# Decode's convolution rows on ScalarE's queue, and a last norm summed on two engines with whole-row stores

## The chip, the cores and the metric

The kernel runs on one core of a Trainium2 chip. The core has TensorE for matrix products (PE in the profile; its weight loads are PEld), VectorE (DVE), ScalarE (ACT), GpSimd (POOL) and SyncE (SP), and 16 DMA engines that all queues share. The metric is the device time of one execution in microseconds; 0.3% of it is about 8 us. Each engine works through its own list of instructions in order; a transfer is started by an instruction in the list ("queue") of the engine that issues it, here SyncE, ScalarE or GpSimd.

## What is computed

One step of a small hybrid decoder with two layers: 1040 prompt tokens (16 learned meta tokens and 1024 of the prompt) and 8 decode tokens, model width 1024. Layer 0 has a causal convolution of width 31, layer 1 an RWKV-7 time mixing; each is followed by a squared-ReLU MLP of width 4096. Two parts of the reference matter here, the convolution's state and the final norm:

```
def _conformer_conv(h, buf, ...):
    u = h @ w_pw1 + b_pw1
    u = u[..., :D_MODEL] * jax.nn.sigmoid(u[..., D_MODEL:])
    full = jnp.concatenate([buf.astype(u.dtype), u], axis=1)
    c = lax.conv_general_dilated(full, w_dw[:, None, :], ...) + b_dw
    ...
    return out, full[:, -CONV_BUF:]

def _rmsnorm(x, g):
    y = xf * lax.rsqrt(jnp.mean(xf * xf, axis=-1, keepdims=True) + RMS_EPS)
    return (y * g.astype(jnp.float32)).astype(x.dtype)

    return (_rmsnorm(h, norm_final), ...)
```

For each of the 8 decode sequences the new convolution state is the old one's last 29 rows, each of 1024 numbers, and one new row. `y_prompt` and `y_sample` are the final norm's output, without the meta tokens.

## The kernel before

All activations lie with channels on the 128 partitions: a tile `h` of `[128, 8, n]` holds 1024 channels (8 tiles of 128, index `k` or `m`) of `n` tokens. The tokens are cut into groups, three for layer 0 (`G0`, 352, 348, 348 tokens), four for the time mixing, and three for the last stage (`G2`: 328, 352, 352 tokens, the meta tokens left out). Matrix products with the big weights are done as three products of split operands (`mm3`, lines 186 to 190): the high part of the weights times the high part of the activations, low times high, and high times low. So each weight block of 512 KB is loaded by SyncE into one of five `raw` buffers (`load_raw`, line 147), copied by ScalarE to its high part (line 158), and GpSimd subtracts to get the low part (line 163). Loads are issued as buffers come free.

The MLP (`mlp`, lines 319 to 388) walks over 32 blocks of the hidden width. For a block `j`, `inp` makes `ps_in` on PE, VectorE scales it (line 343), ScalarE squares it (344) and casts the high part `hh` (141), VectorE makes the low part `hl` (142). For two blocks together, `out` makes eight products `out` that VectorE adds to the residual `h` (355). PE thus needs ScalarE's weight casts and its `hh` all the time.

Between the PE work of the MLP, `filler` hands out other work in portions: generators yield a number for the work they have just traced, and each call of `fill` takes as much as the call's share of a budget. In layer 0's group 0 such a stream is `conv_states` and `conv_dec` (line 549): decode's convolution. `conv_dec` loads the old states of four sequences at a time into a tile `sdec` (line 553; 120 rows of 4 KB on 120 partitions), and then for each `m` transposes them on PE (`pw`, line 559), copies them to `win` on ScalarE (561), multiplies (563), sums (566) and adds the bias (567). In the same loop body, and with no other tie to it than the loop, one sequence's 29 rows are stored to the output from `sdec` (line 564); such a store waits only for the load of its `sdec`.

The planner of the framework works out the order of the instructions of each engine ahead of the run, from the order in which they are traced, their dependences and its own estimate of times; an instruction that is ready may go ahead of earlier ones that are not. In a few sections the order of one engine is fixed by hand (`manual_schedule`): TensorE's in the time mixing and the first group of the last stage, VectorE's in layer 0's last group.

The last stage ends as follows. Group 0 is done on its own; groups 1 and 2 share the weight loads of one MLP. When group 1's last `out` is traced, `done(1)` makes its final norm, `final(1)`, the filler of group 2's last products; `final(2)` comes after everything. `final(g)` (line 1574) sums the squares of the 1024 channels of each token, multiplies `h` by the norm's weights (1587, 1589), transposes to rows of tokens on PE (`pf`, 1613), scales each row by its reciprocal root on ScalarE or VectorE while it is moved to `ot` (1616, 1618), and stores. A group has three blocks of up to 128 tokens. For group 0 the squares are summed by `mean_parts` (line 217): ScalarE squares the eight tiles, GpSimd adds the four even ones and VectorE the four odd ones, and PE sums the two results over the partitions with a column of ones (`fs`, line 1597). For groups 1 and 2 ScalarE writes eight square tiles `fq` (1585), and PE sums all eight over the partitions, 8 matmuls a block. The rows are stored in halves of 512 columns, each after its own eviction (1620 for the prompt, 1622 for the decode tokens, which are in group 2's last block).

Of the kernel before, what the change touches and what calls it, by code (L numbers as in the profile page):

```python
# [8 lines left out]
F32 = mybir.dt.float32  # L9
F32R = mybir.dt.float32r  # L10
BF16 = mybir.dt.bfloat16
AF = mybir.ActivationFunctionType
# [4 lines left out]
P = 128  # L17
D = 1024
KT = D // P
# [7 lines left out]
CB = CW - 1  # L27
# [21 lines left out]
def hybrid_step(tc, x_prompt, x_sample, state_conv, state_shift, state_wkv, meta_tokens,  # L49
# [8 lines left out]
    nc = tc.nc  # L58
    ctx = ExitStack()
    with ctx:  # L60
        def pool(stack, name, bufs, **kw):
            return stack.enter_context(tc.tile_pool(name=name, bufs=bufs, reuse_waits="tile", **kw))
# [4 lines left out]
        ones_d = consts.tile([P, P], F32, name="ones_d")  # L67
# [41 lines left out]
        for name, ap in vecs:  # L109
            n = ap.shape[0]  # L110
# [7 lines left out]
        def vec(name, i):  # L118
            c = col[name] + i
            return pvec[:, c:c + 1]  # L120

        cur = {}
# [7 lines left out]
        def stat(name, tag, bufs, w=None):  # L130
            return cur["stat"].tile([P, w or cur["n"]], F32, name=name, tag=tag, bufs=bufs)
# [60 lines left out]
        def bank(name, tag="mm"):  # L192
            return cur[tag].tile([P, 512], F32, name=name, tag=tag)
# [20 lines left out]
        def tt(name, tag):  # L214
            return cur["tmp"].tile([P, cur["n"]], F32, name=name, tag=tag)

        def mean_parts(src, n, name, square, tag="acc"):

            accs = []
            for i, eng in enumerate((nc.gpsimd, nc.vector)):  # L220
                acc = stat(f"acc_{name}{i}", f"{tag}{i}", 1)
                ks = range(i, KT, 2)
                for j, k in enumerate(ks):
                    if square:
                        d = tt(f"sq_{name}{k}", "t1") if j else acc
                        nc.scalar.activation(d[:, :n], src[:, k, :n], AF.Square)
                        d = d[:, :n]
                    else:
                        d = src[:, k, :n]
                    if j:  # L230
                        eng.tensor_add(acc[:, :n], acc[:, :n] if square or j > 1 else src[:, ks[0], :n], d)
                accs.append(acc)
            return accs
# [156 lines left out]
        with ExitStack() as l0:  # L390
# [6 lines left out]
            actp = [pool(l0, f"actp0{i}", 1) for i in range(2)]  # L397
# [151 lines left out]
            def conv_dec(c, c_col):  # L549

                sd = [decp.tile([P, D], F32, name=f"sdec{i}", tag="st", bufs=2)[:4 * CB, :] for i in range(2)]
                for i in range(2):
                    nc.sync.dma_start(sd[i], state_conv[0, 4 * i:4 * i + 4].rearrange("b w d -> (b w) d"))
                yield 1
                for m in range(KT):
                    win = decp.tile([P, DEC, CW], F32, name=f"win{m}", tag="win")
                    ps = bank(f"pw{m}", "x")
                    for i in range(2):
                        nc.tensor.transpose(ps[:, i * 4 * CB:(i + 1) * 4 * CB], sd[i][:, m * P:(m + 1) * P],
                                            ident[:4 * CB, :4 * CB])  # L560
                    nc.scalar.copy(win[:, :, :CB], ps[:, :DEC * CB].rearrange("p (b w) -> p b w", b=DEC))
                    nc.gpsimd.tensor_copy(win[:, :, CB:CW], udec[:, m, :].unsqueeze(2))
                    nc.vector.tensor_mul(win, win, wdw[:, m:m + 1, :].broadcast_to([P, DEC, CW]))
                    nc.sync.dma_start(o_conv_sample[0, m, 0:CB - 1, :], sd[m // 4][m % 4 * CB + 1:(m % 4 + 1) * CB])
                    rd = decp.tile([P, DEC], F32, name=f"rd{m}", tag="rd")
                    nc.vector.tensor_reduce(rd, win, axis=AX.X, op=ALU.add)
                    nc.scalar.activation(c[:, m, c_col:c_col + DEC], rd, AF.Identity, bias=vec("b_dw", m))
                    yield 1
# [116 lines left out]
            with ExitStack() as s:  # L685
# [39 lines left out]
                for i, parts in enumerate((((1, rwkv_w1[0]), (4, rwkv_a1[0])), ((5, rwkv_g1[0]),))):  # L725
                    own, prev = (xin.tile([P, D], F32, name=f"lr{i}{s_}", tag="xt").rearrange("p (k c) -> p k c", k=KT) for s_ in "op")
                    w = P // len(parts)
                    for q, (j, src) in enumerate(parts):
                        cs = slice(q * w, (q + 1) * w)
# [84 lines left out]
        wide = pool(ld, "wided", 4)  # L814
# [722 lines left out]
        with ExitStack() as l1:  # L1537
            open_tmp(l1, N2, "2", 3, False)
            open_weights(l1, 0, {"w": 5}, "f")
            actp = pool(l1, "actp1", 1)  # L1540
# [33 lines left out]
            def final(g):  # L1574
                lo, n = G2[g]
                hv = hl[g][:, :, :n]
                if g:
                    accs = [(actp, actp2)[g - 1].tile([P, cur["wide"]], F32R, name=f"fq{g}{k}", tag=f"acth{k}").bitcast(F32)
                            for k in range(KT)]
                else:  # L1580
                    accs = mean_parts(hv, n, f"f{g}", True, "facc")
                    yield 3
                for k in range(KT):
                    if g:
                        nc.scalar.activation(accs[k][:, :n], hv[:, k, :], AF.Square)
                    if k % 2:
                        nc.scalar.activation(hv[:, k, :], hv[:, k, :], AF.Copy, scale=vec("norm_final", k))
                    else:
                        nc.vector.tensor_scalar(hv[:, k, :], hv[:, k, :], vec("norm_final", k), None, op0=ALU.mult)
                    if k == 3:  # L1590
                        yield 2
                starts = range(0, n, P)
                ps = bank(f"fs{g}", "x")
                for j, i in enumerate(starts):
                    w = min(P, n - i)
                    for q, acc in enumerate(accs):
                        nc.tensor.matmul(ps[:w, j:j + 1], acc[:, i:i + w], ones_d[:, 0:1], start=q == 0, stop=q == len(accs) - 1)  # L1597
                ss = stat(f"os{g}", "os", 1, 4)
                whole = n // P
                for w, js in ((P, slice(0, whole)), (n % P, slice(whole, len(starts)))):  # L1600
                    if js.stop > js.start:
                        nc.scalar.activation(ss[:w, js], ps[:w, js], AF.Sqrt, bias=eps_t[:w, 0:1])
                        nc.vector.reciprocal(ss[:w, js], ss[:w, js])
                yield 2
                for j, i in enumerate(starts):
                    w = min(P, n - i)
                    c = lo - META + i
                    np_ = max(0, min(w, SEQ - c))
                    ot = (outp if g < 2 else cur["raw"]).tile([P, D], F32, name=f"ot{g}_{i}", tag="raw")
                    for hf in range(2):  # L1610
                        pt = bank(f"pf{g}{i}{hf}", "w" if g < 2 or hf else "mm")
                        for q in range(4):
                            nc.tensor.transpose(pt[:w, q * P:(q + 1) * P], hv[:, hf * 4 + q, i:i + w], ident)
                        cs = slice(hf * 512, (hf + 1) * 512)
                        if hf:
                            nc.scalar.activation(ot[:w, cs], pt[:w, :], AF.Copy, scale=ss[:w, j:j + 1])
                        else:
                            nc.vector.tensor_scalar(ot[:w, cs], pt[:w, :], ss[:w, j:j + 1], None, op0=ALU.mult)
                        if np_:
                            nc.sync.dma_start(o_y_prompt[0, c:c + np_, cs], ot[:np_, cs])  # L1620
                        if np_ < w:
                            nc.sync.dma_start(o_y_sample.rearrange("b t d -> (b t) d")[:, cs], ot[np_:w, cs])
                    yield 5

            def until(last):
# [35 lines left out]
            residp2, actp2, hidp2 = pool(l1, "resid2", 2, **right), pool(l1, "actp2", 1, **right), pool(l1, "hidp2", 2, **right)  # L1661
# [3 lines left out]
            for _ in rest:  # L1665
                pass
            g1 = group(1, actp, hidp, sums)
            fill, rest = filler(2 * KT + MLP2_POINTS, ([ranked(FN, final(0))], FB))
            add, sums = sums_of(2)
            mixer_out(2, residp2, actp2, fill, add)  # L1670
            end = []

            def done(g):
                end.append(filler(KT, ([final(g)], 24)))
# [4 lines left out]
            for it in (rest, end[0][1], final(2)):  # L1679
                for _ in it:  # L1680
                    pass
# [31 lines left out]
```

## Time and profile before

| | us |
|---|---|
| median of 3 runs | 2752.41 |
| lowest and highest run | 2744.53, 2752.92 |
| profiled execution | 2749.91 |
| its span | 2748.2 |
| PE busy | 2641.3 |
| PEld busy | 2480.3 |
| VectorE busy | 1716.6 |
| GpSimd busy | 1443.8 |
| ScalarE busy | 1122.1 |

The profiled execution's time is 1.7 us longer than its span, from the first recorded event to the last. A timeline row gives start and duration in us, engine, line of the kernel, operation, output and inputs with their shapes, a count, and in brackets the engine's idle time before it and what ended it. SPq, ACTq and POOLq are the queues in which an engine's transfers are issued; the duration of such a row is how long the issue held that queue, not how long the transfer took. A matmul in this number format is recorded as one or several passes, and a row with a count merges neighbours.

### The profile page before, as it was taken

The numbers are of one execution on the slowest core, as the hardware profiler recorded it, in microseconds if no ns is written. First come the engines' busy times: TensorE is split into PE (matmuls) and PEld (weight loads), VectorE is DVE, ScalarE is ACT, GpSimd is POOL, SyncE is SP. The second block draws the span as 40 slices with busy tenths as digits, with TensorE's granted clock in tenths as the row PEclk, the third lists the DMA queues.
The fourth block names the chain that finished last, engine by engine and source line by source line (L and its number), as shares of the span: only waits on it lengthen the run. The fifth ranks groups of instructions, "written<-read, shape, count | busy, mean of one in ns | idle before, by whom it ended". The sixth has DMA issues, their size and how long they took to land. (4 is left out here: it accounts for less than half of the span.)

```text
span 2748.2 us, 51718 instructions
## 1 busy us (share of the span) xinstructions
PE 2641.3 (96%) x19948; PEld 2480.3 (90%) x19948; DVE 1716.6 (62%) x3546; ACT 1122.1 (41%) x2095; POOL 1443.8 (53%) x2054
## 2 busy tenths in 40 slices
PE   8999799999999999999999999979999999999998
PEld 8999699999999999877787787769999899999998
DVE  6999699997445345244757457576679753344433
ACT  5546345444444333333434444444543532222222
POOL 6678578878878776022111112365678663333330
PEclk9999899999999999999999999989999999999999
DMA  6663444554447442667777787786776642222211
GB/s 183 172 187 109 130 139 122 157 172 142 138 139 208 138 139 85 199 191 194 200 188 206 190 195 174 186 219 163 193 224 182 168 131 71 69 70 70 70 47 43
DMA packets 625548, 412.30 MB, mean 150 GB/s; under 512 B 121679, under 2 KB 567311, under 8 KB 625301
## 3 DMA queue, kind: packets, MB, share of 16 engines
q1 hardware_dynamic: 544643, 359.55, 46.7%
q10 hardware_dynamic: 72130, 23.61, 4.1%
q0 software_dynamic: 8528, 25.83, 2.9%
q8 instruction: 157, 2.57, 0.4%
q14 instruction: 90, 0.74, 0.1%
HBM read 344.81 MB, written 64.07 MB: 149 GB/s over the span
## 5 line engine op out<-in xcount | busy, mean ns | idle before, releaser
L163 POOL TENSOR_TENSOR wo_lo<-wo_raw,wo_hi 128x256 fp32r<-128x256 f32 x736 | 544.1, 772 | 318.7 <-ACT wo_hi L158 315.7
L163 POOL TENSOR_TENSOR wi_lo<-wi_raw,wi_hi 128x256 fp32r<-128x256 f32 x640 | 472.2, 770 | 264.8 <-ACT wi_hi L158 257.3
L188 PE MATMUL out<-hh,wo_hi 128*128 128x352 f32 (+2 forms) x1536 | 502.1, 327 | 20.3 <-DVE hl L142 13.3
L190 PE MATMUL ps_in<-m_l,wi_hi 128*128 128x352 f32 (+2 forms) x1536 | 494.2, 322 | 4.9 <-DVE m_l L286 4.8
L188 PE MATMUL ps_in<-m_h,wi_hi 128*128 128x352 f32 (+2 forms) x1536 | 495.4, 323 | 0.6 <-ACT m_h L285 0.6
L189 PE MATMUL out<-hh,wo_lo 128*128 128x352 f32 (+2 forms) x1536 | 495.6, 323 | 0.0
L190 PE MATMUL out<-hl,wo_hi 128*128 128x352 f32 (+2 forms) x1536 | 494.6, 323 | 0.0
L189 PE MATMUL ps_in<-m_h,wi_lo 128*128 128x352 f32 (+2 forms) x1536 | 491.9, 320 | 0.0
L355 DVE TENSOR_TENSOR h<-h,out 128x352 f32<-128x352 f32 (+2 forms) x768 | 385.7, 511 | 163.9 <-PE out L190 161.8
L536 DVE SCALAR_TENSOR_TENSOR cv<-u,wdw,cv 128x348 f32<-128x348 f32 (+2 forms) x720 | 377.9, 574 | 0.7
L158 ACT CAST wo_hi<-wo_raw 128x1024 fp32r<-128x1024 f32 x184 | 192.8, 1048 | 342.8 <-PE out L190 165.8
L158 ACT CAST wi_hi<-wi_raw 128x1024 fp32r<-128x1024 f32 x160 | 167.7, 1048 | 396.4 <-PE out L190 197.5
L188 PEld LDWEIGHTS out<-hh,wo_hi 128*128 128x128 f32 x1536 | 292.5, 190 | 27.3 <-DVE hl L142 15.4
L190 PEld LDWEIGHTS ps_in<-m_l,wi_hi 128*128 128x128 f32 x1536 | 288.8, 188 | 9.1 <-DVE m_l L286 8.6
L189 PEld LDWEIGHTS out<-hh,wo_lo 128*128 128x128 f32 x1536 | 291.7, 190 | 0.8
L188 PEld LDWEIGHTS ps_in<-m_h,wi_hi 128*128 128x128 f32 x1536 | 289.8, 189 | 2.6 <-ACT m_h L285 1.1
L190 PEld LDWEIGHTS out<-hl,wo_hi 128*128 128x128 f32 x1536 | 290.8, 189 | 0.2 <-DVE hl L142 0.2
L189 PEld LDWEIGHTS ps_in<-m_h,wi_lo 128*128 128x128 f32 x1536 | 289.2, 188 | 0.7
L343 DVE SCALAR_TENSOR_TENSOR ps_in<-ps_in,rs_m 128x352 f32<-128x352 f32 (+2 forms) x192 | 100.5, 524 | 247.6 <-PE ps_in L190 247.2
L142 DVE TENSOR_TENSOR hl<-ps_in,hh 128x352 fp32r<-128x352 f32 (+2 forms) x192 | 98.7, 515 | 139.7 <-ACT hh L141 139.6
L906 PE MATMUL pv<-mx,wv_raw 128*128 128x256 f32 (+2 forms) x512 | 133.1, 406 | 6.7 <-ACT rk L1082 4.7
L344 ACT ACTIVATE ps_in<-ps_in 128x352 f32<-128x352 f32 (+2 forms) x192 | 85.1, 444 | 132.1 <-DVE ps_in L343 131.7
(363 smaller groups left out, 4701.5 us busy)
## 6 DMA issues: line engine op xcount, KB each, us to landing
wi_raw<-in_w_mlp_in_dram SPq DMA_DIRECT2D x160, 512.0 KB
wo_raw<-in_w_mlp_out_dram SPq DMA_DIRECT2D x160, 512.0 KB
wk_raw<-in_rwkv_w_k_dram SPq DMA_DIRECT2D x32, 512.0 KB
wr_raw<-in_rwkv_w_r_dram SPq DMA_DIRECT2D x32, 512.0 KB
wv_raw<-in_rwkv_w_v_dram SPq DMA_DIRECT2D x32, 512.0 KB
d_ab<-ab POOLq DMA_DIRECT2D x32, 512.0 KB, 4.9
pg_raw<-in_conv_w_pw_dram SPq DMA_DIRECT2D x24, 512.0 KB
pa_raw<-in_conv_w_pw_dram SPq DMA_DIRECT2D x24, 512.0 KB
```

What stands on the lines that cost most here:

```text
L142: eng_lo.tensor_sub(lo, src, hi.bitcast(F32))
L158: nc.scalar.copy(hi[:, :a * b], raw[:, :a * b])
L163: eng_lo.tensor_sub(lo[:, cs], raw[:, cs], hi[:, cs].bitcast(F32))
L188: nc.tensor.matmul(ps, w[0], act[0], start=first, stop=False)
L189: nc.tensor.matmul(ps, w[1], act[0], start=False, stop=False)
L190: nc.tensor.matmul(ps, w[0], act[1], start=False, stop=last)
L343: nc.vector.scalar_tensor_tensor(s, s, 0.0, rs()[:, :n], op0=ALU.max, op1=ALU.mult)
L344: nc.scalar.activation(s, s, AF.Square)
L355: nc.vector.tensor_add(hv[:, 4 * i + m, :], hv[:, 4 * i + m, :], ps[:, :n])
L536: nc.vector.scalar_tensor_tensor(acc[m][:, :n], ug[:, m, j:j + n], wdw[:, m, j:j + 1], acc[m][:, :n], op0=ALU.mult, op1=ALU.add)
L906: nc.tensor.matmul(ps[:, :n], w[:, k, :], act[k], start=k == 0, stop=k == KT - 1)
```

## The change

Three edits. In `conv_dec` the store of a sequence's 29 rows is issued by ScalarE and not by SyncE. In `final` groups 1 and 2 sum their squares as group 0 does, with `mean_parts`, so that two accumulated tiles are left for PE and not eight; a `yield 3` behind it is now taken for every group. And a block's rows are stored whole, once both halves are in `ot`.

```
@@ conv_dec
-                    nc.sync.dma_start(o_conv_sample[0, m, 0:CB - 1, :], sd[m // 4][m % 4 * CB + 1:(m % 4 + 1) * CB])
+                    nc.scalar.dma_start(o_conv_sample[0, m, 0:CB - 1, :], sd[m // 4][m % 4 * CB + 1:(m % 4 + 1) * CB])
@@ final
-                if g:
-                    accs = [(actp, actp2)[g - 1].tile([P, cur["wide"]], F32R, name=f"fq{g}{k}", tag=f"acth{k}").bitcast(F32)
-                            for k in range(KT)]
-                else:
-                    accs = mean_parts(hv, n, f"f{g}", True, "facc")
-                    yield 3
+                accs = mean_parts(hv, n, f"f{g}", True, "facc")
+                yield 3
                 for k in range(KT):
-                    if g:
-                        nc.scalar.activation(accs[k][:, :n], hv[:, k, :], AF.Square)
                     if k % 2:
...
-                        nc.tensor.matmul(ps[:w, j:j + 1], acc[:, i:i + w], ones_d[:, 0:1], start=q == 0, stop=q == len(accs) - 1)
+                        nc.tensor.matmul(ps[:w, j:j + 1], acc[:, i:i + w], ones_d[:, 0:1], start=q == 0, stop=q == 1)
...
-                        if np_:
-                            nc.sync.dma_start(o_y_prompt[0, c:c + np_, cs], ot[:np_, cs])
-                        if np_ < w:
-                            nc.sync.dma_start(o_y_sample.rearrange("b t d -> (b t) d")[:, cs], ot[np_:w, cs])
+                    if np_:
+                        nc.sync.dma_start(o_y_prompt[0, c:c + np_, :], ot[:np_, :])
+                    if np_ < w:
+                        nc.sync.dma_start(o_y_sample.rearrange("b t d -> (b t) d"), ot[np_:w, :])
```

`mean_parts`, which the change calls for all groups (`tt(..., "t1")` is one of three buffers, `stat` one buffer a tag):

```
        def mean_parts(src, n, name, square, tag="acc"):
            accs = []
            for i, eng in enumerate((nc.gpsimd, nc.vector)):
                acc = stat(f"acc_{name}{i}", f"{tag}{i}", 1)
                ks = range(i, KT, 2)
                for j, k in enumerate(ks):
                    if square:
                        d = tt(f"sq_{name}{k}", "t1") if j else acc
                        nc.scalar.activation(d[:, :n], src[:, k, :n], AF.Square)
                        d = d[:, :n]
...
                    if j:
                        eng.tensor_add(acc[:, :n], acc[:, :n] if square or j > 1 else src[:, ks[0], :n], d)
                accs.append(acc)
            return accs
```

## The prediction

> **What bounds the kernel now.** I read the page first: span 2748.2 us, and the shares of the engines. TensorE's matmul row is 96% busy, so nearly everything that is moved on other engines is covered by it, and the change can only be worth something where TensorE stands still or does the work that is taken away.
>
> ```profile
> span 2748.2 us, 51718 instructions
> PE 2641.3 (96%) x19948; PEld 2480.3 (90%) x19948; DVE 1716.6 (62%) x3546; ACT 1122.1 (41%) x2095; POOL 1443.8 (53%) x2054
> PE   8999799999999999999999999979999999999998
> ```
>
> Idle PE is 2748.2 − 2641.3 = 107 us in the whole span, and the slices show one early hole: the fifth (275 to 344 us) is a 7. That is where decode's convolution rows are stored. Next I read the timelines of SyncE's queue, ScalarE and PE there, then the busy times by window.
>
> ```profile
> 292.93 3.28 SPq L564 DMA_DIRECT2D out_dram<-sdec  x3
> 296.32 4.98 SPq L147 DMA_DIRECT2D wi_raw<-in_w_mlp_in_dram  x1
> 301.35 14.54 SPq L564 DMA_DIRECT2D out_dram<-sdec  x4
> 316.00 7.01 SPq L147 DMA_DIRECT2D wo_raw<-in_w_mlp_out_dram  x2
> ...
> SPq L564 <- DMA sdec<-in_state_conv_dram: 3.0, 1, 3.0
> ...
> 306.69 0.34 ACT L561 COPY win<-pw 128x240 f32<-128x240 f32 x1
> 316.26 1.04 ACT L158 CAST wi_hi<-wi_raw 128x1024 fp32r<-128x1024 f32 x1 [9.23 <-PE pw L559]
> ...
> 317.69 0.45 ACT L141 CAST hh<-ps_in 128x352 fp32r<-128x352 f32 x1
> 335.49 1.04 ACT L158 CAST wo_hi<-wo_raw 128x1024 fp32r<-128x1024 f32 x1 [17.35 <-DMA wo_raw<-in_w_mlp_out_dram]
> ...
> 318.75 0.43 PE L188 MATMUL out<-hh,wo_hi 128*128 128x352 f32 x1 [2.61 <-DVE hl L142]
> ...
> 320.90 0.66 PE L188 MATMUL out<-hh,wo_hi 128*128 128x352 f32 x1 [0.91 <-DVE h L355]
> ...
> 337.88 0.66 PE L559 MATMUL pw<-ident,sdec 120*128 120x120 f32 x2 [14.85 <-ACT win L561]
> ...
> 320.50:341.00 20.50, 5.25 (x18) 4.79 (x19) 6.08 (x14) 3.25 (x6) 4.39 (x7) 0.50 0.49 146
> ```
>
> The eight stores of line 564 hold SyncE's queue: the last four for 14.54 us. The weight loads behind them start late and land late, ScalarE stands 17.35 us at the head of its queue for `wo_raw`, and PE idles 2.61 + 0.91 + 14.85 = 18.4 us. Columns of the last row are PE, PEld, DVE, ACT, POOL busy, granted clock, DMA share, GB/s: the clock is 0.50 for the 20.5 us that follow, so its 18 matmuls take 5.25 us where about 0.16 us each (2.9 us) would do: 2.3 us more. **The hole costs 20.7 us.** Why the stores are slow stands in the DMA view of 305 to 313 us, in which almost nothing but them runs:
>
> ```profile
> DMA packets 55, 0.23 MB, mean 29 GB/s; under 512 B 2, under 2 KB 2, under 8 KB 54
> q1 hardware_dynamic: 54, 0.21, 6.5%
> ```
>
> 6.5% of 16 engines is 1.04 engines: each store of 29 rows runs on one engine, 54 packets of mostly 4 KB in 8 us, about 0.155 us a row, so 4.5 us a store and 36 us for eight. Weight loads queue behind them for their share on that engine.
>
> At the other end I read the last 30 us on PE, ScalarE, VectorE and SyncE's queue.
>
> ```profile
> 2716.79 3.42 PE L1597 MATMUL fs<-ones_d,fq 128*128 128x1 f32 x34
> ...
> 2735.60 0.73 PE L1613 MATMUL pf<-ident,h 128*96 128x128 f32 x5
> 2736.17 3.43 PE L1597 MATMUL fs<-ones_d,fq 128*128 128x1 f32 x34
> ...
> 2733.27 0.91 ACT L1585 ACTIVATE fq<-h 128x352 f32<-128x352 f32 x2
> ...
> 2739.63 0.41 ACT L1602 ACTIVATE os<-fs,eps_t 128x2 f32<-128x2 f32 x2 [4.83 <-PE fs L1597]
> ...
> 2741.70 0.74 DVE L1618 TENSOR_SCALAR ot<-pf,os 96x512 f32<-96x512 f32 x1
> ...
> 2732.26 11.14 SPq L1620 DMA_DIRECT2D out_dram<-ot  x6
> 2743.46 0.63 SPq L1622 DMA_DIRECT2D out_dram<-ot  x1
> 2744.18 0.60 SPq L1620 DMA_DIRECT2D out_dram<-ot  x1
> 2744.83 0.32 SPq L1622 DMA_DIRECT2D out_dram<-ot  x1
> ...
> 2720.10:2723.50 3.40, 3.40 (x16) 3.33 (x16) 1.49 (x4) 1.31 (x4) 0.00 (x0) 0.50 0.00 0
> ```
>
> In groups 1 and 2 PE itself sums the squares, 3 blocks by 8 tiles in 48 records of some 0.1 us; 34 of them stand in one row, 3.42 and 3.43 us. In group 1 that row delays the last `ps_in`, and the clock is at 0.50 for the 3.4 us after it; in group 2 everything that follows waits for it.
>
> **The change part by part.** *Stores off SyncE's queue:* SyncE loses eight issues, so loads are issued when their buffers come free. Gain at most the whole hole, −20.7. A buffer's load was issued some 15 us ahead of its cast (the one issued at 316.00 was cast at 335.49, late), so a wait for one store (4.5 us) on the shared engine would be covered.
>
> *Stores onto ScalarE's queue:* they still need 36 us of one engine, and an issue can hold the engine that makes it. ScalarE's own earlier issues show that:
>
> ```profile
> 162.67 0.69 ACTq L721 DMA_DIRECT2D d_ab<-zt  x1
> ...
> 163.40 3.02 ACTq L721 DMA_DIRECT2D d_ab<-zt  x2
> 166.46 2.74 ACTq L722 DMA_DIRECT2D d_v<-zt  x1
> 169.23 0.44 ACTq L723 DMA_DIRECT2D d_v<-zt  x1
> 169.72 0.55 ACT L513 ACTIVATE sg<-ps_g,pvec 128x348 f32<-128x348 f32 x1 [7.12 <-DMA d_ab<-zt]
> ```
>
> ScalarE's next activation stood 7.12 us behind four to six issues. Behind the new ones stand weight casts (line 158), the squaring and `hh` cast that feed PE (344, 141) and decode's own `win` copy (561). How long is ScalarE held? On SyncE the eighth issue was over at 315.89, and the `wo_raw` queued right behind the stores landed at 335.49; less 1.3 us for its own share (a sixteenth of 512 KB at 4 KB per 0.155 us) some 18 us, four stores, were still to run. So a queue lets some four stores run ahead. All eight were issued as early as their rows allowed, in two bursts of four; I expect the same on ScalarE. The first burst then costs little, the second about 36 − 18 = 18 us. From below it costs 0 (issues spread between other work); from above 23 us, if four weight loads run in between at 1.3 us each. The stores' wait for their `sdec` rows (3.0 us on SyncE) moves along and lies inside these bounds. ScalarE may stop for 9 us before PE does: its last instruction ended at 307.03, PE ran on to 316.1. So PE loses 18 − 9 = 9 us, and some 3 for restarting at half clock as now: +12. Above: after 318.1, with the buffers drained, PE ran on for only 4.9 us, so 23 − 5 + 3 = 21. **Net of the first edit −8.7 us, between −20.7 and 0**; I take a value nearer the upper end because the bursts are what this trace shows.
>
> The Trainium skill, "DMA: Bandwidth & Descriptors", section "Why a DMA increments its semaphore by 16 and not by 1", gives the largest divisor up to 16 common to both sides' slowest dimension as the number of engines, so 29 rows get one. The trace agrees (1.04 engines).
>
> *Squares of groups 1 and 2:* ScalarE's eight squares stay. Added are three adds on GpSimd and three on VectorE per group; removed are 18 of 24 matmuls, 36 of 48 records. Group 0 already works so:
>
> ```profile
> L231 POOL TENSOR_TENSOR acc_f<-acc_f,sq_f x3: 892/899/1157, 2152.5 to 2158.7; 128x328 f32<-128x328 f32 x3
> L231 DVE TENSOR_TENSOR acc_f<-acc_f,sq_f x3: 486/1035/1039, 2155.3 to 2158.9; 128x328 f32<-128x328 f32 x3
> L1597 PE MATMUL fs<-ones_d,acc_f x12: 166/250/250, 2253.8 to 2254.8; 128*128 128x1 f32 x8, 128*72 128x1 f32 x4
> ...
> 2700.00:2720.00 20.00, 0.00 (x0) 1.00 0.00 1
> ```
>
> The last row is GpSimd's: 0.00 busy, so it is free. The last two squares run from 2733.27 to 2734.18; one add behind (0.9 to 1.2 on GpSimd, 0.5 to 1.0 on VectorE) both sums stand by 2735.2, before PE has done its transposes (2736.2). So the adds are hidden; without that cover they would cost about 1 us, and another 1 if a square has to wait for one of the three `t1` buffers. Twelve records take 1.1 us (2253.8 to 2254.8), so of 34 in a row 1.2 us remain. Group 2: 3.43 − 1.2 = **−2.2 us**, from −2.5 to +1. Group 1: 36 × 0.1 = 3.6 us of PE work, and the dip of the clock (at full clock those 3.4 us are 1.7 us of work) perhaps too: up to −5.3. But the pause between the last `ps_in` and `hh` is about 2 us and is then less filled, and `yield 3` puts the transposes one call later: **−4 us**, from −5.3 to 0.
>
> *Whole rows:* the last eight issues become four. In time SyncE's tail ends with 2744.83 + 0.32 = 2745.15; the last eviction ends at 2742.44, so two issues behind (a block's and the sample's, 0.6 and 0.3) give 2743.4: up to −1.7. Against that the last transfer has 8 rows of 4 KB on an engine and not of 2 KB: 8 × 0.155 − 0.65 = +0.6. **−1.1 us**, from −1.7 to +0.6.
>
> Sum: −8.7 − 4 − 2.2 − 1.1 = −16.0. The profiled execution took 2749.91 us (span 2748.2 and 1.7 around it): **2733.9 us**. That execution lies 2.5 below the median of the runs, 2752.41, which reach from 2744.53 to 2752.92.
>
> **The rivals.**
> *A, the issues cost ScalarE nothing:* they are spread over its 41% busy stream, and the whole hole goes: 2749.9 − 20.7 − 7.3 = 2721.9. For it speaks ScalarE's idle time, against it the bursts on SyncE.
>
> *B, the bottleneck is the one engine, whichever queue issues:* loads still wait for their share there, or ScalarE's hold is as long as the wait it replaces. First edit 0: 2742.6. For it speaks that the engine needs 36 us in any case; against it that PE's loss came from loads standing behind all stores in one queue. In the DMA view of 166.5 to 168.5 us, both queues move at once:
>
> ```profile
> q1 hardware_dynamic: 832, 0.42, 76.6%
> q10 hardware_dynamic: 327, 0.08, 18.7%
> ```
>
> The Trainium skill, "DMA: Bandwidth & Descriptors", section "Issuing engines are not separate DMA queues", is this rival: it says that another issuing engine only saves the sequencer's time. Its section "Queues, rings and completion order" speaks against: engines alternate between queues packet by packet. These rows bear the second out.
>
> *C, slower: ScalarE is held for the stores' whole time.* If its queue lets fewer than two stores run ahead, all 36 us and six loads in between, 8 us, hold the casts: 44 − 5 + 3 = 42 us lost for 20.7 saved, 7.3 saved at the end: +14.0, 2763.9. It decides from a hold of about 36 us on. Against it: ScalarE let a 256 KB issue go in 0.69 us (162.67) right behind another. For it: the 2.74 us for one small transfer in a full queue.
>
> *D, the end gains nothing:* summing on two engines is late and PE waits in order for it; 7.3 is lost, 2741.2.
>
> **How the numbers follow.** Forecast 0.41, A 0.22, B 0.20, C 0.12, D 0.05. About 0.3% (8 us) is what a measurement can tell from no change. Faster by more: most of the forecast (0.34), A (0.21), a third of B, half of D: 0.64. Within: the rest of these, 0.24. Slower: C, 0.12. For the range: A with all ends at the end of the kernel gives 2749.9 − 20.7 − 9.5 = 2719.7; upward B with no gain at the end reaches 2750; I take 2719 to 2753, which leaves out C and a little of A.
>
> **What would show it.** SyncE's queue has no issue above 1 us between 290 and 340 us, loads of line 147 included. ScalarE's queue has eight issues of line 564; the last three over 3 us each, PE's idle in the fifth slice about 10 us and not 18. If all are under 1 us, A; if ScalarE shows over 30 us of issues, C. At the end `fs` has 12 records a group, no clock dip near 2720, and four issues after the last evictions. The prediction is wrong if the order in which the planner puts the later instructions, which it works out anew, moves more than these 16 us.

## The result, and the profile after

| | before | after |
|---|---|---|
| median of the runs, us | 2751.8 | 2741.97 |
| lowest and highest | 2744.53, 2752.92 | 2740.19, 2747.14 |
| profiled execution, us | 2749.91 | 2744.21 |
| its span, us | 2748.2 | 2742.5 |

The ratio after to before is 0.9972, 95% interval 0.9962 to 0.9983: 0.28% faster, some 8 us (the medians differ by 9.8), about half of the 16 that were forecast. By the experiments below all of it comes from the second edit; the first and the third gave nothing that can be measured.

The page of after: its span, TensorE's row, and TensorE's share by slices of 69 us. The fifth slice is a 7 as it was before, so the hole is still there.

```profile
span 2742.5 us, 51583 instructions
...
PE 2639.7 (96%) x19876; PEld 2478.7 (90%) x19876; DVE 1718.1 (63%) x3552; ACT 1121.1 (41%) x2095; POOL 1449.8 (53%) x2060
...
PE   9999799999999999999998999989999999999998
```

To compare the hole between kernels I use the busy times of one window, 290 to 340 us: PE, PEld, VectorE, ScalarE and GpSimd with their instructions, then the granted clock, the DMA share and GB/s. First before, then after.

```profile
290.00:340.00 50.00, 31.08 (x182) 29.77 (x181) 28.28 (x62) 12.21 (x22) 20.79 (x31) 0.81 0.35 105
```

```profile
290.00:340.00 50.00, 31.52 (x175) 30.61 (x175) 26.53 (x58) 12.36 (x21) 19.96 (x31) 0.76 0.33 103
```

PE has done 175 instructions in the window and not 182, at a slightly lower clock. The hole has not become smaller. What fills it has changed; the timeline of ScalarE in after, its issues (ACTq) and its work in one list:

```profile
290.39 5.12 ACTq L564 DMA_DIRECT2D out_dram<-sdec  x4
295.63 1.05 ACT L158 CAST wi_hi<-wi_raw 128x1024 fp32r<-128x1024 f32 x1 [6.41 <-DMA sdec<-in_state_conv_dram]
296.95 0.23 ACTq L564 DMA_DIRECT2D out_dram<-sdec  x1
297.23 0.45 ACT L344 ACTIVATE ps_in<-ps_in 128x352 f32<-128x352 f32 x1 [0.55 <-DMA sdec<-in_state_conv_dram]
297.25 7.86 ACTq L564 DMA_DIRECT2D out_dram<-sdec  x1
305.15 0.45 ACT L141 CAST hh<-ps_in 128x352 fp32r<-128x352 f32 x1 [7.48 <-issue]
305.18 10.93 ACTq L564 DMA_DIRECT2D out_dram<-sdec  x2
316.15 0.45 ACT L541 COPY u<-cv 128x348 f32<-128x348 f32 x1 [10.54 <-issue]
```

The eight issues hold ScalarE for 5.12 + 0.23 + 7.86 + 10.93 = 24.1 us between 290.39 and 316.11. In its order the `hh` cast of line 141 stands behind the sixth store and the copy of line 541 behind the eighth. On PE and in the view of waits (engine and line, what it waited for: total, times, longest) this is seen from the other side:

```profile
306.22 0.66 PE L188 MATMUL out<-hh,wo_hi 128*128 128x352 f32 x1 [7.64 <-DVE hl L142]
...
319.59 0.66 PE L188 MATMUL out<-hh,wo_hi 128*128 128x352 f32 x1 [10.85 <-DVE h L355]
```

```profile
PE out L188 <- DVE h L355: 10.8, 1, 10.8
...
ACT u L541 <- issue: 10.5, 1, 10.5
DVE cv L533 <- ACT u L541: 10.0, 1, 10.0
```

PE's first stop of 7.64 us waits for `hl`, which needs `hh`. The second, 10.85 us, waits for an addition to `h` (355) on VectorE; VectorE, in order, waits for the convolution's input `u` (533), and `u` for the last issue. Together 18.5 us; before they were 18.4. SyncE's queue, on the other hand, is free, as foretold: a load of `wi_raw` is issued in the midst of it in 0.39 us, and no other issue of line 147 between 285 and 345 us took longer.

```profile
292.13 0.39 SPq L147 DMA_DIRECT2D wi_raw<-in_w_mlp_in_dram  x1
```

The stores' rows ran from 291.5 to 335.5 us, 44 us and not the 36 reckoned with. The reason is seen in the DMA views of 290 to 295.6 us and of 300 to 304 us, with packets, MB and share of 16 engines for each queue (q10 carries the stores now, q1 the loads).

```profile
q1 hardware_dynamic: 1749, 1.30, 84.2%
q10 hardware_dynamic: 11, 0.05, 3.8%
```

```profile
DMA packets 45, 0.10 MB, mean 25 GB/s; under 512 B 0, under 2 KB 23, under 8 KB 45
...
q10 hardware_dynamic: 22, 0.09, 5.5%
q1 hardware_dynamic: 23, 0.01, 1.0%
```

In the first 5.6 us 1.30 MB of loads go by, and of the stores only 11 rows, where from the first one at 291.5 us 4.1 / 0.155 = 26 would have fitted. Then 22 packets of stores and 23 of loads pass in 4 us, together 6.5% of 16 engines and so again about one engine: it takes a packet of each in turn, and a row of a store takes 4 / 22 = 0.18 us and not 0.155. A load pays more for this. Its packets are small (0.01 MB for 23) and each waits for a row, so that the load issued at 292.13 had its last packets at 307.8 us. Nothing in the view of waits from 285 to 345 us waits for it.

In the last stage the rows do what the edit says. The timeline of after, with PE's rows of `fs` for groups 1 and 2, ScalarE's wait for the last of them, and SyncE's last issues; behind it the window around group 1's sums:

```profile
2717.95 0.28 PE L1591 MATMUL fs<-ones_d,acc_f 128*128 128x1 f32 x2
2719.25 1.07 PE L1591 MATMUL fs<-ones_d,acc_f 128*128 128x1 f32 x10
...
2729.76 0.38 PE L1591 MATMUL fs<-ones_d,acc_f 128*128 128x1 f32 x2
2731.98 1.17 PE L1591 MATMUL fs<-ones_d,acc_f 128*128 128x1 f32 x10
...
2733.19 0.41 ACT L1596 ACTIVATE os<-fs,eps_t 128x2 f32<-128x2 f32 x2 [1.20 <-PE fs L1591]
...
2721.73 14.79 SPq L1614 DMA_DIRECT2D out_dram<-ot  x6
2736.57 1.10 SPq L1616 DMA_DIRECT2D out_dram<-ot  x1
```

```profile
2714.00:2724.00 10.00, 10.00 (x73) 9.94 (x72) 6.28 (x14) 5.59 (x14) 0.94 (x1) 1.00 0.13 52
```

12 records a group and not 48, no dip of the clock, and a wait of 1.20 us where 4.83 were. For the worth of each part I take three marks on PE that every kernel has: the three neighbouring passes of line 190 that end a block of `out` (once before and once behind group 1's sums), and the last three transposes. Before, then after:

```profile
2706.52 0.64 PE L190 MATMUL out<-hl,wo_hi 128*128 128x352 f32 x3
...
2726.24 0.73 PE L190 MATMUL out<-hl,wo_hi 128*128 128x352 f32 x3
...
2739.46 0.53 PE L1613 MATMUL pf<-ident,h 128*128 128x128 f32 x3
```

```profile
2707.99 0.64 PE L190 MATMUL out<-hl,wo_hi 128*128 128x352 f32 x3
...
2722.05 0.64 PE L190 MATMUL out<-hl,wo_hi 128*128 128x352 f32 x3
...
2733.01 0.53 PE L1607 MATMUL pf<-ident,h 128*128 128x128 f32 x3
```

| | before | after | difference |
|---|---|---|---|
| start to first mark (the hole is in it) | 2706.52 | 2707.99 | +1.5 |
| first to second mark (group 1's sums) | 19.72 | 14.06 | −5.7 |
| second to third mark (group 2's sums) | 13.22 | 10.96 | −2.3 |
| third mark to the end of the span (stores) | 8.74 | 9.49 | +0.8 |
| span | 2748.2 | 2742.5 | −5.7 |

### The profile page after: what moved, and what is told of

Read it like the earlier page. It is cut to its first block, busy times and chain, and to the rows that moved or that the text cites. A ratio compares the mean times of both kernels' runs of the same rounds, so it can differ in the third digit from the quotient of the medians.

```text
span 2742.5 us, 51583 instructions
## 1 busy us (share of the span) xinstructions
PE 2639.7 (96%) x19876; PEld 2478.7 (90%) x19876; DVE 1718.1 (63%) x3552; ACT 1121.1 (41%) x2095; POOL 1449.8 (53%) x2060
## 5 line engine op out<-in xcount | busy, mean ns | idle before, releaser
L188 PE MATMUL out<-hh,wo_hi 128*128 128x352 f32 (+2 forms) x1536 | 502.8, 327 | 35.5 <-DVE hl L142 18.4
L188 PEld LDWEIGHTS out<-hh,wo_hi 128*128 128x128 f32 x1536 | 293.1, 191 | 42.3 <-DVE hl L142 20.6
```

The source lines that it names most:

```text
L188: nc.tensor.matmul(ps, w[0], act[0], start=first, stop=False)
```

## The experiments

Each starts from the kernel before. Differences are medians against the kernel before on the same chip in the same session.

**One edit at a time.** The first edit alone:

```
-                    nc.sync.dma_start(o_conv_sample[0, m, 0:CB - 1, :], sd[...])
+                    nc.scalar.dma_start(o_conv_sample[0, m, 0:CB - 1, :], sd[...])
```

> The first edit alone. Theory H (a store's issue holds the queue that makes it until about four stores or fewer are still to run, so the hole only moves from late loads to late casts): PE stands some 18 us between 290 and 325 us as in the changed kernel, and the time is that of the kernel before within 3 us. Rival P (my predicted terms; the -8.7 us are there, but in the profiled execution something else lost them): 7 to 11 us faster than before.

Measured: 2750.54 us against 2749.42, ratio 1.0005 (0.9995 to 1.0015, 11 runs). The edit is worth nothing that can be measured. The window and, in the timeline, the two stops of PE are like those of after: 9.61 + 11.01 = 20.6 us idle.

```profile
290.00:340.00 50.00, 29.38 (x167) 28.52 (x166) 25.07 (x55) 12.35 (x21) 18.63 (x29) 0.76 0.34 102
```

```profile
306.20 0.66 PE L188 MATMUL out<-hh,wo_hi 128*128 128x352 f32 x1 [9.61 <-DVE hl L142]
...
319.74 0.66 PE L188 MATMUL out<-hh,wo_hi 128*128 128x352 f32 x1 [11.01 <-DVE h L355]
```

The second edit alone, the sums:

```
...
+                accs = mean_parts(hv, n, f"f{g}", True, "facc")
+                yield 3
                 for k in range(KT):
-                    if g:
-                        nc.scalar.activation(accs[k][:, :n], hv[:, k, :], AF.Square)
```

> The second edit alone, squares of groups 1 and 2 summed on GpSimd and VectorE. By the comparison of the two traces' last additions to h: 5 to 7 us faster than before, with 12 records of fs a group and no dip of the clock near 2720 us. Rival (the gain at the end is mostly the whole-row stores): 0 to 3 us faster.

Measured: 2740.15 us against 2749.42, −9.3 us, ratio 0.996 (0.9946 to 0.9974, 5 runs). This is the whole gain of the change. Two other comparisons agree, in which the sums are all or nearly all that differs: after gained 9.8 us against its kernel before and the first edit alone lost 1.1, which leaves some −11; and the cut stores below take 2728.7 us alone and 2718.78 with sums and whole rows, −9.9.

The third edit alone, whole rows:

```
...
+                    if np_:
+                        nc.sync.dma_start(o_y_prompt[0, c:c + np_, :], ot[:np_, :])
+                    if np_ < w:
+                        nc.sync.dma_start(o_y_sample.rearrange("b t d -> (b t) d"), ot[np_:w, :])
```

> The third edit alone, whole rows stored. Working of the prediction: 1 us faster (0 to 1.7), four issues behind the last evictions. Rival (the last transfer is longer and waits for both halves): 0 to 1 us slower.

Measured: 2750.4 us, ratio 1.0001 (0.9992 to 1.001, 11 runs). Nothing. The DMA view of the last 9 us, before and with whole rows:

```profile
q1 hardware_dynamic: 806, 1.44, 45.9%
```

```profile
q1 hardware_dynamic: 403, 1.44, 44.9%
```

Half the packets, the same 1.44 MB, and the same share of the engines' time. From the third mark to the end the kernels with half rows need 8.74 (before), 9.19 (the sums alone) and 10.47 us (the first edit alone), those with whole rows 9.49 (after) and 9.30 (this one): no order by the size of the stores. Fewer issues do let SyncE end sooner: its last issue ended 5.69 us after the third mark before, 4.66 in after. But from there to the end of the span the three kernels with half rows need 3.0, 3.3 and 3.8 us, those with whole rows 4.8 and 4.5.

**What the hole is worth, and to whom it belongs.** Without the stores of line 564, so that the old rows are not written:

```
-                    nc.sync.dma_start(o_conv_sample[0, m, 0:CB - 1, :], sd[...])
+                    pass
```

> The kernel before without the eight stores of line 564: the 29 old rows of each sequence are not written. What the hole is worth: if the stores alone make it, 19 to 21 us faster than before and no PE idle over 3 us between 285 and 345 us. If the loads of the old states or the transposes make part of it, less than 15 us.

Measured: 2724.73 us, −24.7, ratio 0.9907 (0.9893 to 0.992, 4 runs), and in the window PE stands still nowhere and the clock is 1.00:

```profile
290.00:340.00 50.00, 50.00 (x320) 49.87 (x319) 48.15 (x106) 23.11 (x41) 38.51 (x59) 1.00 0.51 146
```

So the hole is all the stores' doing, and the prediction's 20.7 for it was no overestimate. The same can be read inside the stage: VectorE's additions to `h` (line 355) come at the same places in every kernel, and from the first of them (between 279 and 284 us) to those behind the hole this kernel needs 21.7 us less than before, while after needs 0.4 us more. Next, the same bytes cut into 16 and 13 rows, on SyncE and on ScalarE:

```
-                    nc.sync.dma_start(o_conv_sample[0, m, 0:CB - 1, :], sd[...])
+                    for r, e in ((0, 16), (16, CB - 1)):
+                        nc.sync.dma_start(o_conv_sample[0, m, r:e, :], sd[m // 4][m % 4 * CB + 1 + r:m % 4 * CB + 1 + e])
```

> The kernel before, each store cut into rows 0 to 15 and 16 to 28, still on SyncE's queue. If the hole comes from 29 rows running on one engine, the pieces spread over 16 and 13 engines, the issues no longer hold the queue and the hole goes: 20 to 25 us faster than before, as without the stores, no issue of line 564 above 1.5 us. If the number of bytes or of issues makes the hole, no more than 5 us faster (sixteen issues in place of eight).

> The same cut, on ScalarE's queue. Theory H (the holds are the cost, and they come from the single engine): ScalarE is held for 16 issues of 0.3 us or so, about 5 us, less than the 9 us that PE can stand: 18 to 25 us faster than before, within 3 us of the cut stores on SyncE. If stores on ScalarE's queue cost time by themselves, by their place in its order, 10 us or less.

Measured: on SyncE 2728.7 us against 2748.69, −20.0, ratio 0.9928 (0.9914 to 0.9942, 5 runs); on ScalarE 2727.44, −21.3, ratio 0.9925 (0.991 to 0.994, 6 runs). The groups of the issues (shortest, median and longest in ns, first to last in us), on SyncE, then on ScalarE:

```profile
L565 SPq DMA_DIRECT2D out_dram<-sdec x16: 315/358/612, 291.1 to 300.1; - x16
```

```profile
L565 ACTq DMA_DIRECT2D out_dram<-sdec x16: 321/363/581, 288.8 to 297.4; - x16
```

No issue is held above 0.61 us, though all 16 still go out in one burst of 9 us. By the additions to `h` the stage gains 22.4 and 21.7 us. In the packets of the second kernel up to 14 rows of these stores are under way at once; in after they follow one another. Which queue issues them makes no difference once the rows are spread over more engines.

**Is it the one engine's work, or the burst on it?** Four stores on each queue:

```
-                    nc.sync.dma_start(o_conv_sample[0, m, 0:CB - 1, :], sd[...])
+                    (nc.scalar if m < 4 else nc.sync).dma_start(o_conv_sample[0, m, 0:CB - 1, :], sd[...])
```

> The kernel before with the first four sequences' stores (uncut) on ScalarE's queue and the last four on SyncE's. Theory H (a queue lets about four stores run ahead): ScalarE is held some 5 us as by its first burst in the changed kernel, SyncE by its four less than 6 us; both hide, 12 to 22 us faster than before. Theory E (the one engine, busy for 36 us or more whichever queue issues, delays the loads' shares that pass it): PE idle as before, 15 us or more, and the time within 4 us of before.

Measured: 2750.97 us against 2748.69, ratio 1.0003 (0.9993 to 1.0013, 12 runs). A miss: a good part of the hole was expected to go, and none of it did. SyncE's queue and the next cast of `wo_raw` on ScalarE, then the DMA views of 300 to 304 us and of 308 to 318 us:

```profile
294.73 14.98 SPq L564 DMA_DIRECT2D out_dram<-sdec  x4
...
333.20 1.04 ACT L158 CAST wo_hi<-wo_raw 128x1024 fp32r<-128x1024 f32 x1 [20.15 <-DMA wo_raw<-in_w_mlp_out_dram]
```

```profile
q10 hardware_dynamic: 22, 0.09, 5.5%
q1 hardware_dynamic: 22, 0.01, 0.9%
```

```profile
q1 hardware_dynamic: 33, 0.13, 3.2%
q10 hardware_dynamic: 33, 0.13, 3.2%
```

SyncE's four stores stand in their queue behind a load of `wi_raw` issued at 290.68. While ScalarE's stores run, that load gets one small packet through for each of their rows, 22 and 22 in 4 us, and has its last ones at 306.6; the first row of SyncE's stores moves at 306.9. From then on the engine takes a row of each queue in turn, 33 and 33 in 10 us. So the four hold SyncE's queue for 14.98 us as the last four of eight did (14.54), their rows last until 331.5, and the `wo_raw` behind them is cast at 333.20 (before: 335.49). Halving the burst of a queue does not help while the other half takes every second turn of the same engine.

Then the stores uncut but one at a time: moved behind the sums of line 566, each behind a VectorE instruction that writes the edge of its `sdec` again with its own values, so that a store waits for this `m` and the next such write waits for the store. On ScalarE (the second kernel is the same on SyncE):

```
+                    edge = sd[m // 4][:, D - 1:D]
+                    nc.vector.scalar_tensor_tensor(edge, rd[:4 * CB, 0:1], 0.0, edge, op0=ALU.mult, op1=ALU.add)
+                    nc.scalar.dma_start(o_conv_sample[0, m, 0:CB - 1, :], sd[...])
```

> Uncut stores on ScalarE's queue, each made to wait for its sequence's sums (a one-column VectorE instruction that adds 0 times rd to the rows' last column), so that they come one by one, some 7 us apart, and not in bursts. The single engine is as busy as in the changed kernel; only the holds are gone. Theory H (the hold of the issuing engine is the whole cost on ScalarE): no issue above 2 us, PE idle under 4 us between 285 and 345 us, 16 to 22 us faster than before. Theory E (weight loads that share the engine arrive too late): ScalarE waits for wi_raw or wo_raw and the time stays within 8 us of before.

> The same spacing on SyncE's queue. A load then stands behind one store at most (4.5 us) and not behind four: if the order within the one queue is the cost there, 14 to 22 us faster than before; if a load behind any uncut store is too late, less than 8 us.

Measured: 2730.53 us against 2751.01, −20.5, ratio 0.993 (0.9917 to 0.9942, 5 runs), and 2729.12, −21.9, ratio 0.992 (0.9907 to 0.9934, 4 runs). The group of the issues, the window, and the wait that the edit itself brings (window of the waits: 300 to 345 us), of the one on ScalarE:

```profile
L568 ACTq DMA_DIRECT2D out_dram<-sdec x8: 228/233/241, 305.9 to 460.4; - x8
```

```profile
290.00:340.00 50.00, 44.65 (x268) 43.68 (x267) 41.72 (x92) 19.32 (x33) 32.56 (x49) 0.94 0.47 139
```

```profile
DVE sdec L567 <- DMA out_dram<-sdec: 8.0, 2, 4.3
```

The eight stores still run on one engine, and no issue is held above 0.24 us. PE's idle time in the window falls from 18.9 to 5.4 us, and part of what is left comes from VectorE waiting 8.0 us for stores because of the added write. By the additions to `h`, the profiled executions of both kernels gain 11 us in this stage, half of the 22 without the stores; the rest of the differences of their spans lies before the stage (3.3 and 4.7 us) and behind it (3.3 and 6.5 us), where single executions of the other kernels differ by up to 4 us. So the runs suggest that about all of the hole goes, and the traces show half; where the rest comes from is open. At least half of the cost is thus not the engine's total of some 36 us, but that many stores at once are in front of something.

**Versions that beat both.** Cut stores on SyncE with the sums and whole rows, and the same with half rows:

> The changed kernel with the cut stores on SyncE's queue in place of the uncut ones on ScalarE's: both gains together, 28 to 36 us faster than before, about 2716 us. If the ends of the two stages share a cause (the clock, or the state of the planner's order), less than 26.

> Cut stores on SyncE's queue and squares summed on GpSimd and VectorE, but rows stored in halves as before. As whole rows alone changed nothing, the same time as with whole rows (2718.8) within 3 us; if whole rows pay only where the squares are summed early, 2 us or more slower than that.

Measured: 2718.78 us, ratio 0.9889 (0.9872 to 0.9905, 5 runs), and 2719.43 us, ratio 0.9886 (0.9871 to 0.9901, 4 runs). The two gains add up: −20.0 for the cut and −9.3 for the sums make 2719.4 from the 2748.69 of the first one's session. Whole rows add nothing here either: the two ratios differ by 0.0003, with intervals ten times as wide.

## Why the prediction was right or wrong

*The hole.* Its size (20.7, in the stage 21.7), its cause on SyncE's queue and its removal from there were right. Where PE's new stops would come from was right too: ScalarE held by its own issues.

*The first edit: the step that failed.* The prediction put ScalarE's hold so: "The first burst then costs little, the second about 36 − 18 = 18 us", and from it "So PE loses 18 − 9 = 9 us, and some 3 for restarting at half clock as now: +12", net −8.7. Measured alone the edit is worth +1.1 us (−1.4 to +4.1 by its interval). The slack of 9 us (8.2 here) and the lead of about four stores held. The size of the loss did not, for three reasons:
- The first burst does not cost little: it held ScalarE for 5.12 us. The lead is a little under four stores (the eighth issue was let go at 316.11 with some 110 rows, 3.8 stores, still to move by the packets after it), so the fourth issue already had to wait, while the loads left the stores 11 rows.
- The stores' 36 us assumed the engine for themselves. The loads, no longer stuck behind them, ran beside them: from their first row at 291.5 us to 316.11 the stores moved 123 rows in 24.6 us, which alone would take 19.1. The hold was 24.1 us in all. The prediction had 23 as its upper end, and took a lower value.
- Taking hold less slack leaves out what stands behind the held engine. ScalarE let go at 316.11, PE went on at 319.59: 3.5 us for `u`, the convolution, VectorE's addition.

From ScalarE's first issue at 290.39 to 316.11 are 25.7 us; less 8.2 that PE ran on (to 298.58), plus those 3.5, less some 2.5 us of work that PE did between its two stops, makes the 18.5 us of idle time, where the prediction's step gives 9. It was 18.4 before. Of the signs named ahead, the one on ScalarE's queue came (its last three issues took 7.86, 6.10 and 4.80 us, each over 3), and the one on PE, about 10 us idle, did not. What happened is the second half of the rival "the bottleneck is the one engine": ScalarE's hold as long as the wait it replaces. Its first half, that the loads still wait for their share, happened too, but cost nothing that the trace shows: the load of 292.13 was issued in 0.39 us and got its last packets 15.7 us later, not after the 1.3 us of its own share and one store's 4.5, and nothing waited for it.

The Trainium skill's rule that stands beside this rival ("DMA: Bandwidth & Descriptors", section "Issuing engines are not separate DMA queues": another engine only saves the sequencer's time of issuing) gave the right verdict here. The same sentence calls that time usually small; here it is 24.1 us, and on an engine that also computes it is paid by whoever waits for that engine.

*Rivals.* The time that came lies next to what B (2742.6) and D (2741.2) gave. B had both terms nearly right, nothing for the first edit and 7.3 for the end. D's number is chance: it kept the gain of the first edit and gave up that of the end, and the runs show the reverse. That the issues are spread and cost nothing needed another order of the stores: with it forced, at least half of the hole goes and no issue is held, so the mechanism was right and its condition not met. That ScalarE is held for all 36 us did not happen, because nearly four stores run ahead.

*Group 1: right in kind, too small.* −4 was forecast, from −5.3 to 0; the marks show −5.7. The reason for taking less than the end of the range, that the pause before `hh` would be less filled, showed nothing: PE has no gap there (10.00 of 10.00 us busy in 2714 to 2724). And the clock's dip is longer in other executions than in the one profiled before (below), so the gain is larger against them: between the marks the kernels without the sums need 19.7 to 20.2 us where the dip lasts 3.4 us and 21.3 to 21.7 where it lasts 6.8, those with the sums 14.0 to 14.1.

*Group 2: right.* −2.2 forecast, −2.3 measured between the marks; 10 of the 12 records stand in a row, 1.17 us.

*Whole rows: wrong in small.* −1.1 forecast, nothing measured. SyncE's last issue does end about 1 us sooner after the third mark. The term that was too small is the one against it, +0.6 for the longer last transfer: from the last issue to the end the kernels with whole rows need 0.7 to 1.8 us more than the others.

*The sum.* The terms of the end came to −7.3 and measured −9.3 in the runs; the first edit's −8.7 measured +1.1. That the planner's new order might move more than all this did not come true: up to the first mark the whole difference is 1.5 us, and with whole rows alone, where no edit stands ahead of it, the mark comes 3.4 us sooner than before.

## What to carry to other kernels

An issue is not free for the engine that makes it: when the transfers ahead of it crowd on one DMA engine, it can hold the whole list of work of the engine that issues it, so a store on a computing engine's queue should be priced by its hold plus everything queued behind it, up to the engine that sets the end. Before moving such a transfer to another queue, look at how many DMA engines it runs on; here cutting 29 rows into 16 and 13 took the stall away on either queue, and moving it uncut took away nothing. And here single-column matmuls on the engine that sets the end were worth replacing by additions on idle ones for the clock as well as for their own time.

## What the runs showed of the hardware

Two queues with work on one DMA engine were served a packet each in turn, whether the packets were of equal size (33 and 33 in 10 us, 0.13 MB each) or not (22 of 0.09 MB, 23 of 0.01 MB in 4 us). With small packets in one queue and large ones in the other, the queue with the small ones loses most: a load of 512 KB had its last packets 15.7 us after its issue. And a queue let these stores run ahead by a little under four: when the last of the eight issues was over, 114 of their 232 rows had still to move on SyncE's queue before, and 109 on ScalarE's in after.

TensorE's clock fell while the engine was busy by the records. In the kernel with the first edit alone, group 1's row of 34 single-column matmuls and the window behind its start:

```profile
2714.59 4.59 PE L1597 MATMUL fs<-ones_d,fq 128*128 128x1 f32 x34
```

```profile
2716.60:2723.40 6.80, 6.80 (x34) 6.73 (x34) 2.02 (x5) 1.99 (x5) 0.00 (x0) 0.50 0.01 2
```

PE is busy for all 6.80 us and the clock is 0.50, twice as long as in the kernel before (3.4 us, from 2720.10). A dip of one of these two lengths, beginning within this row or up to 1.2 us behind it, stands in the traces of all nine kernels that have it, and in none of the four with the sums on GpSimd and VectorE. The Trainium skill, "TensorE: Matmul & The Clock Gate", section "Part 1: The HAM clock gate (the "warmup" mystery)", says that the clock is halved after an idle window of about 3.4 us. The two lengths, 3.4 and 6.8 us, agree with one and two such windows; that a row of single-column matmuls counts as idle is what these rows suggest beyond it, and no run here varied their number alone.
